# The seam between output projection and feed-forward, rearranged: first weights earlier, late tiles later, pair sums from kept values

## The chip, the cores and the metric

The kernel runs on one core of one Trainium2 chip. The metric is the device time of the whole program in microseconds (us), the median of several runs. One run of it was taken with the hardware profiler; all rows below are of that run.

## The reference

A step through a trunk of two layers, for 256 context tokens and 1024 latent tokens, which the kernel holds together as 1280 tokens in ten tiles of 128 (tiles 0 and 1 are context). Each layer has a mixer (layer 0 gMLP and attention, layer 1 neighbourhood attention) and then a feed-forward part; around each stand RMS norms, shift, scale and gate. What matters here is the end of the mixer and the start of the feed-forward part:

```
y  = mixer_out @ w_out                              # output projection, 1024 x 1024
x  = x + gate * rms_norm(y, norm_mix_post)
h  = rms_norm(x, norm_ffn_pre) * (1 + scale) + shift
g, u = split(h @ ffn_w_in)
out = (silu(g) * u) @ ffn_w_out
```

## The kernel before, in words

**Numbers.** Every matrix product in full precision is three products of rounded operands: a value is split into a high part (a CAST, L173 on VectorE (DVE) or L175 on ScalarE (ACT)) and a low part, the rest (TENSOR_TENSOR, L176, on GpSimd (POOL) or DVE). `hh` and `hl` hold the high and low parts of the normed, transposed tokens.

**Output projection** (`out_proj`, L1125). The tiles come in the order 4, 5, 6, 7, 8, 9, 2, 3, 0, 1; the last two, 0 and 1, are called late. `pipeline` runs four stages over them, each some steps behind the first: `load` (layer 0: the mixer's output is loaded and split, ACT L175 and POOL L176 of 128x1024), `product` (TensorE (PE), L190 to L192, 48 matmuls in layer 0 and 30 in layer 1, into one of two PSUM tiles A), `cols` and `norms`. `norms` is a chain of small steps on three engines, and I name it by its lines: sum of squares of y (ACT L353, then DVE L213), its root (POOL L214, a power, which I call the pow), gate and scale (DVE L431, which also frees A), the sum with x (DVE L432), then a second sum of squares (ACT L353), a second pow (POOL L214), and the normed tile `xh`, called hat here (DVE L359).

`cols` calls `prenorm_pair` (L382). PE transposes the hat in eight pieces (L394), ACT applies scale and shift to each (L397), and the result is split into `hh` and `hl`. The feed-forward products work on pairs of tiles, even and odd, and need sums over the pair. So the odd tile's `cols` has a pair chain behind it: POOL L403 (b - a), the splits, DVE L406 twice (a minus the even tile's high part, then minus its low part), POOL L408, L409 and L410 (the last two again with the even tile's high and low parts), and three stores to `t_d`. `cols` of a tile comes 2 steps behind `load` in layer 0 and 3 steps in layer 1. For the late tiles it is left out there and called inside `ffn`. The code of `out_proj` is put in order by the framework's scheduler, engine by engine.

**Feed-forward** (`ffn`, L1185). A block product is 12 matmuls (`three`, L1183) over four chunks of a weight block and a set of tiles: set 0 is the tiles 4 to 9 (128x384), set 1 the tiles 0 to 3 (128x256). Seven products make one output block; four of them, 1, 5, 2 and 3 (`FREE`), use `hh` and `hl` as they are. I write (m, i, s) for the product i of block m and set s. The first ones are (0,1,0), (0,5,0), (0,2,0), (0,3,0) and then (1,1,0) to (1,3,0). Their weights are loaded (L1213), combined (`weight_sums`) and split (ACT L175, POOL L176). `collect` takes a product out of its PSUM bank, first of all with an ACT COPY (L1266 for i = 1, L1274 for i = 5, L1277 for i = 2 the Silu). Here (0,2,0) adds onto the bank of (0,1,0), so it needs that bank's copy. The order inside `ffn` is written by hand: `at(p, ...)` gives each step a place, and `weave` runs them in the order of p on every engine. The late tiles' `cols` are at 0.04 and 1.45, the products start at 0.3.

Every engine works its instructions off in the program's order, so an instruction that waits holds those behind it on the same engine.

Of the kernel before, what the change touches and what calls it, by code (L numbers as in the profile page):

```python
# [49 lines left out]
def trunk_kernel(ctx: ExitStack, tc: tile.TileContext, A: dict, O: dict):  # L50
# [330 lines left out]

    def prenorm_pair(t, xh, l, w, lo, make, wide):  # L382


# [799 lines left out]

    def ffn(l, ubase, xsrc, dst, extra, before, after=()):  # L1185


# [27 lines left out]
        def weight_sums(m):  # L1215
# [13 lines left out]
            eng.tensor_tensor(s2, s1, g[:, 0], op=ALU.subtract)  # L1229
            if m == 0:  # L1230
                weights(m, 3)
                POOL.tensor_tensor(s3, g[:, 0], u[:, 0], op=ALU.subtract)
# [774 lines left out]
```

## Time and profile before

| | |
|---|---|
| median of 3 runs | 3361.82 us (3358.36 to 3364.49) |
| profiled run | 3360.7 us, span 3358.9 us |
| PE busy | 3166.4 us, 94% of the span, 18370 matmuls |
| DVE, POOL, ACT busy | 58%, 54%, 42% |
| granted clock of PE, mean | 0.974 |

The span is the time from the first to the last instruction of the profiled run. A row of a timeline reads: start in us, duration in us, engine, line and operation, tile written <- tiles read, shapes, count, and in brackets how long the engine had been idle before and which instruction ended that idle time. The granted clock 1.00 is full speed, 2.4 GHz; 0.5 is the lower level of 1.2 GHz; a mean between the two is a mix of stretches at either.

The out_proj and the first products of layer 0 lie at about 590 to 765 us, those of layer 1 at about 2370 to 2503 us.

### The profile page before, as it was taken

How to read it: one execution, taken by the hardware profiler on the slowest of the kernel's cores; microseconds unless marked ns; L12 is line 12 of the kernel's file. 1: busy time of each engine (PE TensorE's matmuls, PEld its weight loads, DVE VectorE, ACT ScalarE, POOL GpSimd, SP SyncE). 2: the span in 40 equal slices, each digit the busy share in tenths (PEclk: the TensorE clock that was granted, in tenths of full speed). 3: DMA queues.
4: the chain of work that ended last, by engine and by line, in shares of the span. 5: the costliest groups of instructions: out<-in, count | busy, mean ns of one | idle time of the engine just before them, and what ended most of it. 6: DMA issues, size and time to landing. Idle time of an engine off the chain costs nothing. (4 is left out here: it accounts for less than half of the span.)

```text
span 3358.9 us, 48818 instructions
## 1 busy us (share of the span) xinstructions
PE 3166.4 (94%) x18370; PEld 2785.2 (83%) x18370; DVE 1933.6 (58%) x3446; ACT 1404.4 (42%) x2935; POOL 1801.9 (54%) x1359
## 2 busy tenths in 40 slices
PE   7899999979999999999899999998869999999998
PEld 4688877759999999887778888887769999998877
DVE  4689988445667665444656666666666322224444
ACT  3478843433222223112456656566442333332121
POOL 4667765567656657434443433335376655565340
PEclk8999999989999999999999999999979999999999
DMA  6200134444233334223211111123443121223233
GB/s 228 78 17 26 45 99 151 140 133 136 101 113 114 130 124 131 89 85 126 106 49 46 48 47 50 46 67 105 135 138 123 62 82 62 69 84 119 83 119 119
DMA packets 167880, 321.14 MB, mean 96 GB/s; under 512 B 13518, under 2 KB 93262, under 8 KB 167644
## 3 DMA queue, kind: packets, MB, share of 16 engines
q1 hardware_dynamic: 167644, 318.03, 29.2%
q8 instruction: 144, 2.36, 0.3%
q14 instruction: 92, 0.75, 0.1%
HBM read 245.46 MB, written 72.52 MB: 95 GB/s over the span
## 5 line engine op out<-in xcount | busy, mean ns | idle before, releaser
L176 POOL TENSOR_TENSOR w<-raw,w 128x512 fp32r<-128x512 f32 (+1 forms) x303 | 463.5, 1540 | 372.9 <-ACT w L175 370.7
L1183 PE MATMUL B<-hh,w 128*128 128x384 f32 (+1 forms) x2112 | 523.2, 323 | 35.0 <-ACT s L1277 17.3
L1183 PE MATMUL A<-s,w 128*128 128x384 f32 (+1 forms) x3168 | 489.7, 310 | 6.1 <-DVE s L1269 6.0
L1183 PEld LDWEIGHTS A<-s,w 128*128 128x128 f32 x3168 | 474.3, 188 | 13.8 <-DVE s L1269 6.7
L1183 PEld LDWEIGHTS B<-hh,w 128*128 128x128 f32 x2112 | 376.9, 192 | 41.2 <-ACT s L1277 18.0
L175 ACT CAST w<-raw 128x512 fp32r<-128x512 f32 (+1 forms) x306 | 201.3, 688 | 459.8 <-DVE raw L1229 282.7
L1183 PE MATMUL B<-hl,w 128*128 128x384 f32 (+1 forms) x1056 | 339.7, 322 | 0.0
L477 PE MATMUL B<-c,s 128*128 128x128 f32 x1344 | 208.9, 279 | 26.7 <-DVE raw L459 14.3
L191 PE MATMUL B<-w,hh 128*128 128x512 f32 x552 | 220.2, 399 | 13.7 <-POOL w L176 13.7
L322 DVE SCALAR_TENSOR_TENSOR t<-s,c,t 128x512 f32<-128x512 f32 x196 | 216.0, 1148 | 25.7 <-DMA s<-mod_w 25.6
L190 PE MATMUL B<-w,hh 128*128 128x512 f32 x552 | 221.2, 401 | 8.4 <-DVE s L1404 8.4
L214 POOL TENSOR_TENSOR sm<-sm,c 128x1 f32<-128x1 f32 (+2 forms) x110 | 86.1, 783 | 266.3 <-DVE sm L213 264.6
L1404 DVE TENSOR_TENSOR s<-s,B 128x512 f32<-128x512 f32 x192 | 132.0, 687 | 161.9 <-PE B L192 161.9
L176 POOL TENSOR_TENSOR hl<-raw,hh 128x640 fp32r<-128x640 f32 (+1 forms) x84 | 127.9, 1526 | 174.3 <-ACT hh L175 166.5
L192 PE MATMUL B<-w,hl 128*128 128x512 f32 x552 | 219.8, 398 | 0.0
L190 PE MATMUL C<-hh,w 128*128 128x512 f32 (+1 forms) x576 | 213.1, 370 | 3.2 <-ACT s L135 1.2
L477 PEld LDWEIGHTS B<-c,s 128*128 128x128 f32 x1344 | 157.4, 142 | 67.6 <-DVE raw L459 17.5
L493 DVE TENSOR_TENSOR t<-B,t 128x512 fp32r<-128x512 f32 (+2 forms) x216 | 127.5, 590 | 143.8 <-ACT t L487 129.8
L192 PE MATMUL C<-hh,w 128*128 128x512 f32 (+1 forms) x576 | 205.9, 357 | 0.3 <-POOL w L176 0.3
L191 PE MATMUL C<-hl,w 128*128 128x512 f32 (+1 forms) x576 | 205.0, 356 | 0.0
L1183 PEld LDWEIGHTS B<-hl,w 128*128 128x128 f32 x1056 | 202.6, 192 | 0.0
L849 POOL TENSOR_TENSOR s<-s,sm 128x640 f32<-128x640 f32 x128 | 156.7, 1254 | 64.4 <-DVE sm L847 45.1
(361 smaller groups left out, 7891.1 us busy)
## 6 DMA issues: line engine op xcount, KB each, us to landing
raw<-wall SPq DMA_DIRECT2D x147, 512.0 KB, 3.6
s<-mod_w SPq DMA_DIRECT2D x56, 512.0 KB, 5.5
raw<-gu_d SPq DMA_DIRECT2D x88, 320.0 KB, 2.8
gu_d<-s SPq DMA_DIRECT2D x44, 384.0 KB, 3.1
raw<-x_d SPq DMA_DIRECT2D x30, 512.0 KB, 3.7
raw<-mod_w SPq DMA_DIRECT2D x24, 512.0 KB, 3.8
gu_d<-s SPq DMA_DIRECT2D x44, 256.0 KB, 3.3
w<-wall SPq DMA_DIRECT2D x22, 512.0 KB, 3.6
```

Of the source, the lines that this page charges most:

```text
L175: ACT.copy(hi, src)
L176: (eng or DVE).tensor_tensor(lo, src, f32(hi), op=ALU.subtract)
L190: PE.matmul(out, sh, mh, start=i == 0, stop=False)
L191: PE.matmul(out, sh, ml, start=False, stop=False)
L192: marks["PE"] = PE.matmul(out, sl, mh, start=False, stop=i == n - 1)
L214: POOL.tensor_tensor(r, v, mhalf[:, 0:n], op=ALU.pow)
L322: DVE.scalar_tensor_tensor(total[c], r[:, b], cond[:, k + b, c : c + 1], total[c], op0=ALU.mult, op1=ALU.add)
L477: PE.transpose(tr[:, at : at + P], self.p[a][:, col : col + P], ident)
L493: DVE.tensor_tensor(tl[:, 0:n], tr[:, 0:n], f32(th[:, 0:n]), op=ALU.subtract)
L849: POOL.tensor_tensor(p[:, c], p[:, c], z.to_broadcast([P, 640]), op=ALU.mult)
L1183: PE.matmul(out, x, z, start=start and i + j == 0, stop=i == n - 1 and j == 2, skip_group_check=True)
L1404: DVE.tensor_tensor(yt, yt, part, op=ALU.add)
```

## The change

Five things change, in both layers.

1. `out_proj` calls `ahead` within the product of the last tile: the first weight block is loaded there, and its weights 1, 5 and 2 are made there, so that the scheduler may set them among the work of the output projection. `ffn` becomes a generator that hands out `ahead`, and `ffn_behind` joins the two.
2. `cols` comes 3 steps behind `load` in both layers (it was 2 in layer 0).
3. In the hand-written order the first products stand at 0.0 (0.3 before), ahead of the late tiles' `cols`, which go to 0.71 and 2.45. The remaining sums of the first weights (`first_sums`) are made at 0.96, three of the four on DVE. Loads and splits of the pair sums move as shown.
4. Where `keep` is set (layer 1; in layer 0 the late tiles only) the even tile's values are kept, so one DVE L413 takes the place of two L406, and one POOL L417 that of L409 and L410.
5. The low part of b (the odd tile's second half) is always made on POOL; the low part of block 1's weights 5 and 3 goes to DVE.

Lines move by about ten: L403 becomes L409, L406 becomes L413, L408 becomes L415, L409 and L410 become L419 and L420 (or L417), L419 becomes L429, L431 becomes L441, L1183 becomes L1195, L1266 becomes L1289.

```diff
-    def prenorm_pair(t, xh, l, w, lo, make, wide):
+    def prenorm_pair(t, xh, l, w, lo, keep, wide):
...
             split(hh[:, :, rows(t)], hl[:, :, rows(t)], xh, lo, DVE)
+            if keep:
+                st["even"] = xh
             return
...
-        POOL.tensor_tensor(more[:, 0], b, a, op=ALU.subtract)
-        split(hh[:, 4:8, rows(t)], hl[:, 4:8, rows(t)], b, lo, DVE)
-        for x in (hh, hl):
-            DVE.tensor_tensor(a, a, f32(x[:, 0:4, rows(t - 1)]), op=ALU.subtract)
+        POOL.tensor_tensor(more[0], b, a, op=ALU.subtract)
+        split(hh[:, 4:8, rows(t)], hl[:, 4:8, rows(t)], b, POOL, DVE)
+        even = st.pop("even") if keep else None
+        for x in [even] if keep else (f32(hh[:, :, rows(t - 1)]), f32(hl[:, :, rows(t - 1)])):
+            DVE.tensor_tensor(a, a, x[:, 0:4], op=ALU.subtract)
         split(hh[:, 0:4, rows(t)], hl[:, 0:4, rows(t)], a, lo, DVE)
         POOL.tensor_tensor(b, b, a, op=ALU.subtract)
-        POOL.tensor_tensor(more[:, 1], f32(hh[:, 4:8, rows(t - 1)]), b, op=ALU.subtract)
-        POOL.tensor_tensor(more[:, 1], more[:, 1], f32(hl[:, 4:8, rows(t - 1)]), op=ALU.add)
+        if keep:
+            POOL.tensor_tensor(more[1], even[:, 4:8], b, op=ALU.subtract)
+        else:
+            POOL.tensor_tensor(more[1], f32(hh[:, 4:8, rows(t - 1)]), b, op=ALU.subtract)
+            POOL.tensor_tensor(more[1], more[1], f32(hl[:, 4:8, rows(t - 1)]), op=ALU.add)
...
+            if t == OUT_ORDER[-1]:
+                ahead()
...
-            prenorm_pair(t, st.pop(("xh", t)), l, 1, DVE if early else POOL, wt if early and t not in late else s5, t in late)
+            prenorm_pair(t, st.pop(("xh", t)), l, 1, DVE if early or t in late else POOL, early or t in late, t in late)
-        pipeline(OUT_ORDER, (0, load), (1, product), (3 if early else 2, lambda t: t in late or cols(t)), (1, norms))
+        pipeline(OUT_ORDER, (0, load), (1, product), (3, lambda t: t in late or cols(t)), (1, norms))
...
+        def first_sums():
+            g, u, s0 = st["gu", 0, 0], st["gu", 0, 1], st["s", 0]
+            DVE.tensor_tensor(s0[6], s0[5], g[:, 0], op=ALU.subtract)
+            weights(0, 3)
+            DVE.tensor_copy(s0[4], u[:, 1])
+            POOL.tensor_tensor(s0[7], g[:, 0], u[:, 0], op=ALU.subtract)
...
-            split(o[:, 0], o[:, 1], src, POOL)
+            split(o[:, 0], o[:, 1], src, DVE if m == 1 and i in (5, 3) else POOL)
+        def ahead():
+            weights_load(0)
+            weights(0, 1)
+            weight_sums(0)
+        yield ahead
...
-        at(0.04, before[0])
-        at(0.22, weights_load, 1)
-        p = 0.3
+        at(0.71, before[0])
+        at(0.96, first_sums)
+        at(0.97, weights_load, 1)
+        p = 0.0
...
-        at(1.45, before[1])
+        at(2.45, before[1])
...
-            at(1.7 + 0.25 * j, weights, 1, i)
+            at(2.55 + 0.45 * j, weights, 1, i)
...
-            at(0.5 + 0.7 * j, sums_load, i, h, 0)
-            at(2.6 + 0.7 * j, sums_split, i, h, 0)
+            at(1.2 + 0.7 * j, sums_load, i, h, 0)
+            at(3.6 + 0.6 * j, sums_split, i, h, 0)
```

How it moves instructions shows at three places. First POOL in the output projection of layer 0, in the kernel before. s_1118 is tile 5's hat, both L214 are tile 6's pows, and the last row is the split of a later tile's mixer output.

```order
L214 TENSOR_TENSOR sm_6483<-sm_6482,c_68 128x1
L403 TENSOR_TENSOR s_1126_6465<-s_1118_6388 128x512
L176 TENSOR_TENSOR hl_73<-s_1118_6388,hh_72 128x4x128
L408 TENSOR_TENSOR s_1118_6388<-s_1118_6388 128x512
L176 TENSOR_TENSOR hl_73<-s_1118_6388,hh_72 128x4x128
L409 TENSOR_TENSOR s_1126_6465<-hh_72,s_1118_6388 128x512
L214 TENSOR_TENSOR sm_6494<-sm_6493,c_68 128x1
L410 TENSOR_TENSOR s_1126_6465<-s_1126_6465,hl_73 128x512
L176 TENSOR_TENSOR s_1139_6502<-raw_6499,s_1138_6501 128x1024
```

The chain of the same tile 5 in the changed kernel, where s_1116 is its hat and both L214 are tile 7's pows:

```order
L409 TENSOR_TENSOR t_1141_6542<-s_1116_6368 128x512
L176 TENSOR_TENSOR hl_73<-s_1116_6368,hh_72 128x4x128
L415 TENSOR_TENSOR s_1116_6368<-s_1116_6368 128x512
L176 TENSOR_TENSOR hl_73<-s_1116_6368,hh_72 128x4x128
L419 TENSOR_TENSOR t_1142_6543<-hh_72,s_1116_6368 128x512
L420 TENSOR_TENSOR t_1142_6543<-t_1142_6543,hl_73 128x512
L214 TENSOR_TENSOR sm_6561<-sm_6560,c_68 128x1
L214 TENSOR_TENSOR sm_6572<-sm_6571,c_68 128x1
L176 TENSOR_TENSOR s_1155_6580<-raw_6577,s_1154_6579 128x1024
```

Before, the first of the two pows stands ahead of the odd tile's pair chain and the second within it; now both stand behind all of the chain.

The same holds for the chains of the tiles 7, 9 and 3. PE's order follows: before, a tile's eight transposes stood between two products and no other tile's with them; now, between the products of the tiles 8 and 9, the eight of tile 6 and the first four of tile 7 stand (B_6731 from s_1152, tile 7's hat), and so the product of tile 9 waits for tile 7's hat.

Second, POOL in the output projection of layer 1, before (the L403 is the one of tile 7; the L214 behind it is the pow of tile 9's y; L419 makes the context tiles' gate):

```order
L403 TENSOR_TENSOR w_23262<-s_3678_23134 128x512
L214 TENSOR_TENSOR sm_23280<-sm_23279,c_68 128x1
L408 TENSOR_TENSOR s_3678_23134<-s_3678_23134 128x512
L409 TENSOR_TENSOR w_23262<-hh_72,s_3678_23134 128x512
L410 TENSOR_TENSOR w_23262<-w_23262,hl_73 128x512
L419 TENSOR_TENSOR w_23370<-w_23370,raw_23371 128x1024
```

and in the changed kernel, where s_3683 is tile 7's hat:

```order
L409 TENSOR_TENSOR t_3702_23263<-s_3683_23135 128x512
L176 TENSOR_TENSOR hl_73<-s_3683_23135,hh_72 128x4x128
L415 TENSOR_TENSOR s_3683_23135<-s_3683_23135 128x512
L417 TENSOR_TENSOR t_3703_23264<-s_3667_23050,s_3683_23135 128x512
L429 TENSOR_TENSOR w_23370<-w_23370,raw_23371 128x1024
L214 TENSOR_TENSOR sm_23280<-sm_23279,c_68 128x1
```

The pow of tile 9 moved from behind L403 to behind L417 and the gate's product, L429; the chain has one instruction fewer of its own and one split of b more.

Third, ACT at the start of the first products of layer 0 in the changed kernel. s_1226 and s_1243 are the hats of the tiles 3 and 0, A_7095 is y of tile 1, and the L1289 is the copy that (0,2,0) waits for.

```order
L397 ACTIVATE s_1226_6994<-B_7163,c_74 128x128 x2
L175 CAST w_7156<-t_1249_7151 128x512
L175 CAST w_7159<-raw_7144 128x512
L397 ACTIVATE s_1226_6994<-B_7163,c_74 128x128 x2
L397 ACTIVATE s_1243_7091<-A_7243,c_74 128x128
L353 ACTIVATE t_1259_7195,sm_7196<-A_7095,c_70 128x1024
L397 ACTIVATE s_1243_7091<-A_7243,c_74 128x128 x7
L353 ACTIVATE t_1264_7206,sm_7207<-s_1263_7202,c_70 128x1024
L1289 COPY s_1272_7262<-B_7217 128x384
```

In the kernel before the copy (L1266 there) stands here, behind tile 0's eight L397 but with tile 1's two sums of squares well ahead:

```order
L353 ACTIVATE t_1239_7113,sm_7114<-s_1238_7109,c_70 128x1024
L353 ACTIVATE t_1246_7173,sm_7174<-A_7124,c_70 128x1024
L353 ACTIVATE t_1251_7184,sm_7185<-s_1250_7180,c_70 128x1024
L175 CAST w_7207<-t_1259_7202 128x512
L175 CAST w_7210<-raw_7195 128x512
L1226 COPY t_1262_7205<-raw_7197 128x512
L175 CAST w_7216<-raw_7195 128x512
L397 ACTIVATE s_1243_7120<-A_7220,c_74 128x128 x8
L175 CAST w_7271<-raw_7239 128x512
L175 CAST w_7274<-raw_7239 128x512
L1266 COPY s_1274_7277<-B_7243 128x384
```

Now the copy stands behind tile 1's second sum of squares, that is, behind all of tile 1's `norms`.

## Rows read from the trace of the kernel before

**Rows 1.** Windows: us, busy us of PE, PEld, DVE, ACT, POOL, PEclk, DMA share, GB/s.

```profile
603.81:615.75 11.94, 11.94 (x58) 9.84 (x56) 6.31 (x6) 6.18 (x13) 5.86 (x4) 1.00 0.41 134
631.55:645.18 13.63, 13.63 (x56) 11.25 (x57) 6.15 (x6) 5.09 (x11) 7.94 (x5) 0.87 0.53 161
661.03:676.77 15.74, 15.10 (x56) 11.87 (x57) 6.14 (x6) 5.08 (x11) 7.94 (x5) 0.78 0.50 151
719.25:765.05 45.80, 26.07 (x113) 24.61 (x114) 19.56 (x17) 19.80 (x40) 36.96 (x29) 0.78 0.45 149
2460.00:2503.20 43.20, 23.68 (x97) 21.85 (x97) 23.34 (x20) 18.71 (x38) 33.68 (x24) 0.71 0.44 146
```

**Rows 2.** Timeline of PE, layer 0: start, us, engine, line, tiles [idle before <-releaser].

```profile
631.55 1.86 PE L394 MATMUL B<-c,s 128*128 128x128 f32 x8 [3.69 <-DVE sm L213]
...
661.03 1.09 PE L394 MATMUL B<-c,s 128*128 128x128 f32 x8 [3.74 <-DVE sm L213]
...
723.54 1.64 PE L394 MATMUL A<-c,s 128*128 128x128 f32 x8 [4.29 <-DVE sm L213]
...
739.23 0.69 PE L1183 MATMUL B<-hh,w 128*128 128x384 f32 x1 [6.24 <-ACT s L1266]
...
756.09 0.69 PE L1183 MATMUL B<-hh,w 128*128 128x384 f32 x1 [8.01 <-ACT s L1277]
```

**Rows 3.** Timeline of POOL, layer 0, 646 to 663 us.

```profile
646.91 0.55 POOL L214 TENSOR_TENSOR sm<-sm,c 128x1 f32<-128x1 f32 x1 [4.15 <-DVE sm L213]
649.57 1.48 POOL L403 TENSOR_TENSOR s<-s 128x512 f32<-128x512 f32 x1 [2.11 <-ACT s L397]
651.01 1.30 POOL L176 TENSOR_TENSOR hl<-s,hh 128x512 fp32r<-128x512 f32 x1
...
654.73 1.48 POOL L408 TENSOR_TENSOR s<-s 128x512 f32<-128x512 f32 x1 [2.42 <-issue]
...
657.43 1.26 POOL L409 TENSOR_TENSOR s<-hh,s 128x512 f32<-128x512 f32 x1
...
660.38 2.81 POOL L176 TENSOR_TENSOR s<-raw,s 128x1024 fp32r<-128x1024 f32 x1
```

**Rows 4.** Timeline of ACT, layer 0, 645 to 650 us.

```profile
645.44 1.11 ACT L353 ACTIVATE t<-A,c 128x1024 bf16<-128x1024 f32 x1 [6.44 <-PE A L192]
...
646.54 2.89 ACT L397 ACTIVATE s<-B,c 128x128 f32<-128x128 f32 x8
```

**Rows 5.** Timeline of DVE, layer 0, 649 to 654 us.

```profile
649.81 1.28 DVE L431 SCALAR_TENSOR_TENSOR s<-A,sm,s 128x1024 f32<-128x1024 f32 x1
651.08 1.78 DVE L406 TENSOR_TENSOR s<-s,hh 128x512 f32<-128x512 f32 x1
652.78 1.21 DVE L432 TENSOR_TENSOR s<-s,raw 128x1024 f32<-128x1024 f32 x1
```

**Rows 6.** Timeline of DVE, layer 1: L431 of tiles 7 and 3.

```profile
2397.15 1.28 DVE L431 SCALAR_TENSOR_TENSOR s<-A,sm,w 128x1024 f32<-128x1024 f32 x1 [0.44 <-POOL sm L214]
...
2438.83 1.28 DVE L431 SCALAR_TENSOR_TENSOR s<-A,sm,w 128x1024 f32<-128x1024 f32 x1 [0.44 <-POOL sm L214]
```

**Rows 7.** Timeline of PE, layer 1.

```profile
2398.58 0.47 PE L190 MATMUL A<-s,hh 128*128 128x512 f32 x1 [2.40 <-DVE s L431]
...
2407.13 1.04 PE L394 MATMUL B<-c,s 128*128 128x128 f32 x8
...
2455.17 1.94 PE L394 MATMUL A<-c,s 128*128 128x128 f32 x8 [6.91 <-DVE s L359]
...
2467.23 0.69 PE L1183 MATMUL B<-hh,w 128*128 128x384 f32 x1 [6.05 <-ACT w L175]
...
2477.68 0.44 PE L1183 MATMUL B<-hh,w 128*128 128x384 f32 x1 [3.40 <-ACT s L1266]
...
2495.06 0.69 PE L1183 MATMUL B<-hh,w 128*128 128x384 f32 x1 [9.31 <-ACT s L1277]
```

**Rows 8.** Timeline of POOL, layer 1: the gate's product.

```profile
2422.19 2.87 POOL L419 TENSOR_TENSOR w<-w,raw 128x1024 f32<-128x1024 f32 x1
```

More of the change, by code (lines that the diff above doesn't have):

```diff
@@ L399, in prenorm_pair @@
             split(hh[:, :, rows(t)], hl[:, :, rows(t)], xh, lo, DVE)
+            if keep:
+                st["even"] = xh
             return
         a, b = xh[:, 0:4], xh[:, 4:8]
-        more = make([P, 2, 4, P])
-        POOL.tensor_tensor(more[:, 0], b, a, op=ALU.subtract)
-        split(hh[:, 4:8, rows(t)], hl[:, 4:8, rows(t)], b, lo, DVE)
-        for x in (hh, hl):
-            DVE.tensor_tensor(a, a, f32(x[:, 0:4, rows(t - 1)]), op=ALU.subtract)
+        if wide:
+            more = s5([P, 2, 4, P])
+            more = [more[:, i] for i in range(2)]
+        else:
+            more = [t2([P, 4, P]) for _ in range(2)]
+        POOL.tensor_tensor(more[0], b, a, op=ALU.subtract)
[3 more added lines that the diff above has]
+            DVE.tensor_tensor(a, a, x[:, 0:4], op=ALU.subtract)
         split(hh[:, 0:4, rows(t)], hl[:, 0:4, rows(t)], a, lo, DVE)
         POOL.tensor_tensor(b, b, a, op=ALU.subtract)
-        POOL.tensor_tensor(more[:, 1], f32(hh[:, 4:8, rows(t - 1)]), b, op=ALU.subtract)
-        POOL.tensor_tensor(more[:, 1], more[:, 1], f32(hl[:, 4:8, rows(t - 1)]), op=ALU.add)
-        for i, src in enumerate((b, more[:, 0], more[:, 1])):
+        if keep:
+            POOL.tensor_tensor(more[1], even[:, 4:8], b, op=ALU.subtract)
+        else:
+            POOL.tensor_tensor(more[1], f32(hh[:, 4:8, rows(t - 1)]), b, op=ALU.subtract)
+            POOL.tensor_tensor(more[1], more[1], f32(hl[:, 4:8, rows(t - 1)]), op=ALU.add)
+        for i, src in enumerate((b, *more)):
             SP.dma_start(t_d[l][i][:, :, rows(t // 2)], src)
@@ L1122, in trunk_kernel, with out_proj @@
     finish(mod_part)
-    def out_proj(l, w, xsrc, dst, early=None):
+    def out_proj(l, w, xsrc, dst, early=None, ahead=None):
         w0, w1 = w[:4], w[4:]
@@ L1225, in weight_sums @@
                 weights(m, 2)
-                ACT.copy(a22, u[:, 1])
             else:
                 DVE.tensor_tensor(s3, g[:, 0], u[:, 0], op=ALU.subtract)
[L1229 to L1232, printed above, removed]
+                DVE.tensor_tensor(s2, s1, g[:, 0], op=ALU.subtract)
+        def first_sums():
[4 more added lines that the diff above has]
+            POOL.tensor_tensor(s0[7], g[:, 0], u[:, 0], op=ALU.subtract)
         def weights(m, i):
@@ L1237, in weights @@
             if i == 3:
-                (DVE if m else POOL).tensor_tensor(g[:, 1], g[:, 1], st["s", m][6], op=ALU.subtract)
+                DVE.tensor_tensor(g[:, 1], g[:, 1], st["s", m][6], op=ALU.subtract)
             src = {1: g[:, 0], 2: g[:, 1], 3: g[:, 1]}[i] if i < 4 else st["s", m][i]
             st["w", m, i] = o = wt([P, 2, 512], F32R)
-            split(o[:, 0], o[:, 1], src, POOL)
+            split(o[:, 0], o[:, 1], src, DVE if m == 1 and i in (5, 3) else POOL)
[4 more added lines that the diff above has]
+        yield ahead
         banks = {}
@@ L1303, in both @@
             at(p + (SHORT if s else LONG) + 0.12, collect, m, i, s)
-        at(-0.02, weights_load, 0)
-        at(0.0, weights, 0, 1)
-        at(0.02, weight_sums, 0)
-        at(0.04, before[0])
-        at(0.22, weights_load, 1)
-        p = 0.3
+        at(0.71, before[0])
+        at(0.96, first_sums)
+        at(0.97, weights_load, 1)
+        p = 0.0
         for i in FREE:
@@ L1313, in ffn @@
             p += LONG
-        at(1.45, before[1])
-        at(0.95, weights, 1, 1)
-        at(1.0, weights, 1, 2)
-        at(1.6, weight_sums, 1)
+        at(2.45, before[1])
+        at(1.35, weights, 1, 1)
+        at(1.95, weights, 1, 2)
+        at(2.0, weight_sums, 1)
         for j, i in enumerate((5, 3)):
-            at(1.7 + 0.25 * j, weights, 1, i)
+            at(2.55 + 0.45 * j, weights, 1, i)
         for i in FREE:
@@ L1493, in ffn, with ffn_behind @@
             finish(steps)
-    late_cols = out_proj(0, early_w, lambda t: A["x"][rows(t), :], x_d[0])
+    def ffn_behind(l, *args):
+        k = args.index(None)
+        before = []
+        steps = ffn(l, *args[k + 1 : k + 5], before, *args[k + 5 :])
+        before += out_proj(l, *args[:k], ahead=next(steps))
+        finish(steps)
     FIRST = {0: 0, 7: 640}
@@ L1659, in trunk_kernel @@
     first_units = []
-    ffn(
-        0, U_F0, x_d[0], lambda t: x_d[1][rows(t), :], mods_of((1, 0), (1, 1), (0, 5), (1, 2), (1, 3), (1, 4)), late_cols,
+    ffn_behind(
+        0, early_w, lambda t: A["x"][rows(t), :], x_d[0], None,
+        U_F0, x_d[0], lambda t: x_d[1][rows(t), :], mods_of((1, 0), (1, 1), (0, 5), (1, 2), (1, 3), (1, 4)),
         [first_products(CH[0]), by_turns(first_products(CH[1]), itertools.chain(first_head(0), first_loads()))],
@@ L1889, in trunk_kernel @@
         finish(gen)
-    late_cols = out_proj(1, o_w, lambda t: grid_rows(x_d[1], t), x_d[2], o_sums)
     def last(t):
         return O["yp"][rows(t), :] if t < 2 else O["ys"].rearrange("(r j c) d -> j r c d", j=8, c=8)[t - 2]
-    ffn(1, U_F1, x_d[2], last, mods_of((1, 5)), late_cols)
+    ffn_behind(1, o_w, lambda t: grid_rows(x_d[1], t), x_d[2], o_sums, None, U_F1, x_d[2], last, mods_of((1, 5)))
 def _units_k(w, n):
```

## The prediction

> **What bounds the kernel now.** The table above has PE busy 94% of the span, so only its idle time and its lower clock can be won or lost. The program order differs only around the two seams, so I read those. I took the windows first [rows 1]: an undisturbed step of layer 0's output projection lasts 11.94 us, all of it PE work at granted clock 1.00, while steps around a wait last 13.63 and 15.74 us at 0.87 and 0.78. The first products are worse: PE is busy in 26.07 of 45.80 us in layer 0 and in 23.68 of 43.20 us in layer 1, at 0.78 and 0.71. Then PE's timeline, for what ends the waits. In layer 0 [rows 2] eight transposes wait 3.69 us for the hat of tile 6, and 3.74 for that of tile 8; at the seam stand waits of 4.29, 6.24 and 8.01 us. In layer 1 [rows 7] a product waits 2.40 us for L431 (its PSUM tile A is not free), and at the seam stand 6.91, 6.05 and 9.31. Last POOL, DVE and ACT around such a wait [rows 3 to 5], for what is late: the hat needs two pows, and POOL has them among the pair chain's long instructions. POOL's queue there is what the change rearranges.
>
> **Output projection of layer 0.** Before, products end at 627.86 (tile 7: 631.55 less 3.69), 657.29 (tile 9) and 719.25 (tile 1) [rows 2]. After, with `cols` a step later, one set of transposes fewer stands ahead of tile 7's product: it ends about 1.0 us earlier, at 626.8 (a set takes 1.09 at full clock in [rows 2]).
>
> From there the way to tile 9's product is this. Tile 5's first four transposes and its eight L397 (2.89 [rows 4]): 626.8 + 0.6 + 2.9 = 630.3. Then POOL's pair chain: L409 1.48, split 1.30, L415 1.48, split 1.30, L419 and L420 1.26 each, 8.1 in all; in the trace POOL also stood 2.42 us within a chain [rows 3], beside DVE instructions of the same data [rows 5]. That bounds the chain by 8.1 and 10.5; both cases are equally near, so I take 9.25: 639.6. Only now come the pow of y (0.55 [rows 3]), L441 1.28 and L442 1.21 [rows 5], the second sum of squares (1.11 [rows 4] and some 0.2 of readout), the second pow 0.55, and the split of tile 9's mixer output 2.81 [rows 3]: 647.3, with three or four hand-overs of 0.1 to 0.2, 647.9. Meanwhile tile 8's product has ended at 638.8 and the transposes of tile 6 at 639.8, so PE stands about 6 us for tile 7's hat and 1.5 more for the split. The rest of the product needs 10.5 (11.94 less a set of transposes, less what ran before the split was there): 658.4, plus c for the lower clock after the wait.
>
> The next two odd tiles repeat it: tile 7's chain holds the split of tile 3's mixer output, tile 9's that of tile 1. One period is 0.6 + 2.9 + 9.25 + 7.4 + 0.6 + 10.5 = 31.3 + c. For c the trace has 13.63 - 11.94 = 1.7 and 15.74 - 11.94 = 3.8 [rows 1], of which the second holds 0.6 more idle time; with nothing lost it is 0. I take 1.6. Tile 1's product then ends at 626.8 + 3 x 32.9 = 725.5 against 719.25: **+6** (with 8.1 and 0: -2; with 10.5 and 3.2: +14). So the waits of 3.7 go, and what is late next is the odd tile's pow.
>
> One rule of the Trainium skill bears on the chain ("SBUF — State Buffer", section "Who interferes with whom"): a VectorE instruction with both inputs in SBUF and a GpSimd instruction that reads SBUF block one another whole. The trace agrees: L406 on 512 columns took 1.78 beside POOL's split, longer than L432's 1.21 on 1024 [rows 5]. By that rule the b split, newly on POOL in layer 1, delays the L413 beside it by 0.5 us a chain, some 1.5 us for three chains, and the forecast would be 3373.
>
> **Seam of layer 0**, from the end Z of tile 1's product. The first weights are now ready, so (0,1,0) and (0,5,0) follow at once; the waits of 4.29 and the small ones behind it go. But (0,2,0) needs the bank's copy, and on ACT that stands behind all of tile 1's `norms`, whose pow stands behind tile 3's pair chain on POOL. Z + 0.5 (second half of tile 3's transposes) + 2.7 (four L397 and two casts) + 9.25 + 0.55 + 1.28 + 1.21 + 1.3 + 0.6 for the copy and 1.3 of hand-overs: Z + 18.7. Before it was 739.23 - 719.25 = 20.0 [rows 2]. So the front of the seam gives back 1.3. Behind it, tile 1's transposes now come after (1,1,0), and the cast for (1,5,0) stands behind their L397 on ACT: 2.89 + 0.6 for the copy + 0.6 for the cast + the low part, now on DVE at 0.7 to 1.8, some 5.5 us of new wait. The wait of 8.01 shrinks by less, since the copies of (0,2,0) and (0,3,0) still come one behind the other. I put all PE waits at 12.5 + 1.5 + 5.5 + 2 = 21.5 against 45.80 - 26.07 = 19.7 [rows 1]: **+2** (-1 with the last two terms hidden, +5 with another stretch at the lower clock).
>
> **Output projection of layer 1.** Here `cols` was 3 behind already. L431 of tile 7 started at 2397.15 [rows 6], its pow within tile 5's chain; now the pow is behind L417: one split (1.30) and the rest of the chain later, less the dropped L410: 2399.9. Tile 9's product begins when A is free: 2399.9 + 1.28 + 0.15 = 2401.3, and lasts 8.55 as before [rows 7], since the wait ahead of it is longer: 2409.9. Then 0.6 + 2.9 + 1.3 (a sum of squares stands between tile 7's L397) + the chain of 5.6 (1.48, 1.30, 1.26, 1.5) + the gate's 2.87 [rows 8] + 0.55 + 0.4: L441 of tile 9 at 2424.1. And again, with 1.4 + 7.7 for tile 3's product (8.55, or 6.8 where the clock is granted) and no gate: 20.6, L441 of tile 3 at 2444.7 against 2438.83 [rows 6]: **+6** (+3 with full clock, +7.5 with the lock above).
>
> **Seam of layer 1**, from Y, the start of tile 3's L441. Tile 1's product, tile 3's transposes and (0,1,0) follow without a wait, the last at Y + 9.5; before it came 18 us behind Y, after the 6.91. (0,5,0) still waits: its cast needs the weight sum on POOL, behind the split of tile 3's b, behind eight L397: Y + 9.5 + 2.9 + 1.3 + 1.3 + 1.3 + 1.3 = Y + 17.6, its low part at 20. (0,2,0) needs the copy behind tile 1's norms, and their pow stands behind tile 3's chain: Y + 31.5 (24.6 for the pow, then 1.28, 1.2, 1.3, the late L397 2.5, the copy 0.6), against 2477.68 - 2438.83 = 38.9 [rows 6, 7]. Of these 7.4 about half is given back as in layer 0: set 0's free products end at Y + 61 instead of 2503.20 - 2438.83 = 64.4 [rows 1, 6]: **-3.5** (-6 to -2).
>
> What else changes I cost at nothing. On SP the two weight loads go ahead of the last tiles' transfers, and the late tiles' three stores each come later; the loads of the pair sums that read them come later too, and the products that need these sums lie behind all free products of both sets, well over 20 us on. DVE's new splits stand where PE works on the products before. Without that cover a split costs its 0.7 to 1.8 us once, a late transfer as much as it is late.
>
> **Sum:** 6 + 2 + 6 - 3.5 = +10.5. The profiled run had 3360.7 us (span 3358.9), 1.1 below the median, so I predict about 3371 to 3372.
>
> **Rivals.**
> *The first products fill the waits.* If ACT gets to the copies before tile 1's norms are done, (0,1,0), (0,5,0) and (0,2,0) run back to back. In layer 1 that saves 6.91, 6.05 and most of the 9.31 with their stretches at 0.71, some 18; in layer 0 4.29 and 6.24, some 10; with the output projections at their lower ends (-2, +3): -27, 3335. Half of it gives 3348. For it: the weights are indeed ready early. Against: each engine keeps its order, and the copy stands behind the norms. It decides once POOL's chain of tile 3 ends before tile 1's product does; I have it 12 us later in layer 0.
> *The waits only move.* Chain of 8.1 and little clock loss in layer 0 (+0), seam +1, layer 1 +3 and -4: within 6 us of before, 3361. For it: the cycle of 31.3 is close to the old one, (719.25 - 627.86) / 3 = 30.5.
> *The chain is slow.* 10.5 per chain and c of 3: layer 0 +13, the rest +6: 3381. For it: 2.42 of waiting within a chain was seen.
>
> **Chances.** My forecast 0.41, the slow chain 0.12, moved waits 0.22, filled waits 0.25. A measurement tells about 0.2% (6.7 us) from no change. Faster 0.26 (the filled waits and a little), same 0.24, slower 0.50. For 8 in 10 the range must reach into the filled waits' milder half: 3349 to 3383; the forecast's own is 3364 to 3379.
>
> **What would show it.** In the new profile: POOL's L214 behind L420 with PE's transposes of tile 7 waiting some 6 us; tile 1's product ending near 725; in layer 1 L441 of tile 3 near 2452 (2444.7 and the 8 us of layer 0); (0,2,0) ended by ACT's L1289 in both seams. I am wrong if POOL's pow starts before L419, if PE's waits around the products of the tiles 9 and 3 are under 3 us, or if the seams lose more than 10 us of their idle time.

## The result, and the profile after

The changed kernel takes 3382.82 us (median of 4, 3380.9 to 3384.48), the kernel before 3360.28 in the same comparison: 1.0063 times as long, 95% interval 1.0048 to 1.0078. It is slower, as forecast, and by about twice the forecast amount (22.5 us against 10.5 to 11); 3382.8 lies at the upper end of the stated range and above the forecast's own 3364 to 3379.

The page of the changed kernel, its span and PE's share:

```profile
span 3382.3 us, 48785 instructions
PE 3164.1 (94%) x18370; PEld 2782.2 (82%) x18370; DVE 1914.6 (57%) x3447; ACT 1402.6 (41%) x2933; POOL 1779.4 (53%) x1348
```

PE does the same matmuls in 3164 busy us; the span has grown by 23.4. Where it grew is read from the starts of the same instructions in both traces (us; E6 and E1 are the ends of tile 6's and tile 1's products in layer 0, C the first product of set 1):

| stretch | before | after | difference | forecast |
|---|---|---|---|---|
| start to E6, layer 0 | 615.8 | 610.7 | -5.0 | -1.0 |
| E6 to E1, output projection | 103.5 | 112.2 | +8.7 | +7.3 |
| E1 to C, seam | 47.1 | 49.3 | +2.2 | +2 |
| C to the 601st matmul of the feed-forward | 76.7 | 78.9 | +2.2 | 0 |
| from there to tile 4's transposes, layer 1 | 1536.6 | 1540.3 | +3.7 | 0 |
| these to tile 1's product's end | 67.7 | 79.8 | +12.1 | +6 |
| seam of layer 1 | 57.1 | 52.6 | -4.5 | -3.5 |
| C to the 601st matmul | 75.0 | 78.2 | +3.2 | 0 |
| the rest | 779.4 | 780.3 | +0.9 | 0 |

The fifth row and the last hold no instruction whose order changed; from the first only tile 4's eight transposes are gone, which now stand behind E6 (the forecast's 1.0). Further runs (below) put the first at 611.4 to 617.0 for kernels with these transposes behind E6, and at 613.8 in a second run of the kernel before, so single traces can't tell some 3 us there. That second run has 101.6, 48.1 and 76.9 in the next three rows, and 68.0, 57.5 and 76.3 in those of layer 1; so 1 to 2 us of a row aren't told from scatter either.

PE's timeline in layer 0 of the changed kernel, its waits of more than 1 us from tile 9's product on (this answers to [rows 2]):

```profile
641.99 0.45 PE L394 MATMUL B<-c,s 128*128 128x128 f32 x1 [6.37 <-DVE s L359]
...
673.82 0.79 PE L190 MATMUL A<-s,s 128*128 128x512 f32 x1 [4.64 <-ACT s L175]
...
676.69 0.79 PE L192 MATMUL A<-s,s 128*128 128x512 f32 x1 [1.65 <-POOL s L176]
...
709.26 0.45 PE L394 MATMUL B<-c,s 128*128 128x128 f32 x1 [6.34 <-DVE s L359]
...
741.46 0.69 PE L1195 MATMUL B<-hh,w 128*128 128x384 f32 x1 [12.50 <-ACT s L1289]
...
756.30 0.45 PE L1195 MATMUL B<-hh,w 128*128 128x384 f32 x1 [3.87 <-ACT w L175]
...
762.57 1.01 PE L1195 MATMUL B<-hh,w 128*128 128x384 f32 x2 [5.66 <-DVE w L176]
...
792.66 4.85 PE L1195 MATMUL A<-s,w 128*128 128x384 f32 x14 [4.10 <-DVE s L1292]
```

The waits of 3.7 are gone, and in their place stand 6.37 for tile 7's hat, 4.64 and 1.65 for the split of the mixer's output, 6.34 for tile 3's hat. At the seam (0,2,0) waits 12.50 for the copy, (1,5,0) 3.87 and 5.66 for its cast and its low part. POOL at the first of these waits (it answers to [rows 3]):

```profile
626.26 1.54 POOL L409 TENSOR_TENSOR t<-s 128x512 f32<-128x512 f32 x1 [4.70 <-ACT s L397]
627.76 1.30 POOL L176 TENSOR_TENSOR hl<-s,hh 128x512 fp32r<-128x512 f32 x1
630.48 1.48 POOL L415 TENSOR_TENSOR s<-s 128x512 f32<-128x512 f32 x1 [1.42 <-DVE s L413]
631.91 1.30 POOL L176 TENSOR_TENSOR hl<-s,hh 128x512 fp32r<-128x512 f32 x1
633.17 1.30 POOL L419 TENSOR_TENSOR t<-hh,s 128x512 f32<-128x512 f32 x1
634.55 1.26 POOL L420 TENSOR_TENSOR t<-t,hl 128x512 f32<-128x512 f32 x1
635.78 0.55 POOL L214 TENSOR_TENSOR sm<-sm,c 128x1 f32<-128x1 f32 x1
640.51 0.55 POOL L214 TENSOR_TENSOR sm<-sm,c 128x1 f32<-128x1 f32 x1 [4.18 <-DVE sm L213]
641.25 2.81 POOL L176 TENSOR_TENSOR s<-raw,s 128x1024 fp32r<-128x1024 f32 x1 [0.20 <-ACT s L175]
```

Tile 5's whole chain, L409 to L420, stands ahead of tile 7's first pow at 635.78; the second comes at 640.51, the split at 641.25, and PE goes on at 641.99. POOL's queue isn't alone in this. On DVE the step ahead of the pow, L213, stands behind the chain's steps too, at 630.71, though ACT had the sum ready at 627.3. In more_s5, the first of the experiments, it runs as soon as ACT has it. Both rows, changed kernel first:

```profile
630.71 0.15 DVE L213 TENSOR_SCALAR sm<-sm 128x1 f32<-128x1 f32 x1
```

```profile
627.06 0.15 DVE L213 TENSOR_SCALAR sm<-sm 128x1 f32<-128x1 f32 x1 [2.07 <-ACT t L353]
```

Layer 1 of the changed kernel, PE's waits in the output projection and at the seam, answering to [rows 7]:

```profile
2413.58 0.76 PE L190 MATMUL A<-s,hh 128*128 128x512 f32 x1 [5.66 <-DVE s L441]
...
2439.08 0.76 PE L190 MATMUL A<-s,hh 128*128 128x512 f32 x1 [6.98 <-DVE s L441]
...
2461.33 0.77 PE L190 MATMUL A<-s,hh 128*128 128x512 f32 x1 [4.53 <-DVE s L441]
...
2479.47 0.69 PE L1195 MATMUL B<-hh,w 128*128 128x384 f32 x1 [5.33 <-ACT w L175]
...
2493.20 0.69 PE L1195 MATMUL B<-hh,w 128*128 128x384 f32 x1 [7.67 <-ACT s L1289]
...
2508.36 0.69 PE L1195 MATMUL B<-hh,w 128*128 128x384 f32 x1 [3.87 <-ACT w L175]
2514.62 1.01 PE L1195 MATMUL B<-hh,w 128*128 128x384 f32 x2 [5.26 <-DVE w L176]
```

Here A is not free: three waits for L441 of 5.66, 6.98 and 4.53, where before stood five for L431: 2.40 [rows 7], 1.83, two under 1 and the longest of them:

```profile
2430.37 0.63 PE L190 MATMUL A<-s,hh 128*128 128x512 f32 x1 [2.81 <-DVE s L431]
```

Windows around the idle time and the product behind it, in the changed kernel (a step of layer 0 without a wait first; columns as in [rows 1]):

```profile
610.71:622.65 11.94, 11.94 (x58) 9.85 (x57) 6.30 (x6) 6.18 (x13) 5.86 (x4) 1.00 0.45 133
634.59:656.61 22.02, 15.48 (x61) 12.10 (x60) 7.68 (x10) 9.65 (x20) 11.40 (x8) 0.77 0.45 134
2408.00:2424.00 16.00, 10.42 (x37) 8.40 (x38) 9.98 (x14) 4.81 (x12) 4.64 (x5) 0.79 0.37 113
2434.00:2448.01 14.01, 8.93 (x30) 7.18 (x31) 8.09 (x10) 2.94 (x6) 4.72 (x5) 0.76 0.52 161
2456.80:2471.02 14.22, 9.70 (x31) 7.72 (x31) 10.52 (x12) 5.46 (x13) 5.37 (x6) 0.76 0.34 112
```

A step without a wait still takes 11.94 us at 1.00. Over wait and product together the clock is 0.76 to 0.79, and a product of 30 matmuls, some 6.9 us at full clock, takes 9.7 (2413.58 to the next transposes at 2423.31).

### The profile page after: what moved, and what is told of

Its sections match the earlier page's. It is cut to its first block, busy times and chain, and to the rows that moved or that the text cites. A ratio compares the mean times of both kernels' runs of the same rounds, so it can differ in the third digit from the quotient of the medians.

```text
span 3382.3 us, 48785 instructions
## 1 busy us (share of the span) xinstructions
PE 3164.1 (94%) x18370; PEld 2782.2 (82%) x18370; DVE 1914.6 (57%) x3447; ACT 1402.6 (41%) x2933; POOL 1779.4 (53%) x1348
## 4 chain that ended last, share of the span: by engine, by line
PE 46%; DVE 6%; ACT 4%; POOL 4%; issue 4%; DMA 2%; POOLq 0%; DVEq 0%; SPq 0%; ACTq 0%
PE A L1195 8%; PE B L1195 8%; PE B L191 3%; PE B L192 3%; PE B L190 3%; PE C L190 3%; PE C L192 3%; PE C L191 2%; PE A L190 2%; PE C L1195 2%; PE A L191 2%; PE A L192 2%; PE B L487 2%; PE B L521 2%; POOL w L176 1%
## 5 line engine op out<-in xcount | busy, mean ns | idle before, releaser
L1195 PE MATMUL B<-hh,w 128*128 128x384 f32 (+1 forms) x2112 | 522.0, 323 | 47.2 <-ACT s L1289 20.2
L1195 PE MATMUL A<-s,w 128*128 128x384 f32 (+1 forms) x3168 | 493.1, 312 | 8.5 <-DVE s L1292 8.2
L1195 PEld LDWEIGHTS A<-s,w 128*128 128x128 f32 x3168 | 477.6, 190 | 16.4 <-DVE s L1292 8.8
L1195 PEld LDWEIGHTS B<-hh,w 128*128 128x128 f32 x2112 | 375.4, 191 | 54.4 <-ACT s L1289 20.7
L1195 PE MATMUL B<-hl,w 128*128 128x384 f32 (+1 forms) x1056 | 339.1, 321 | 0.0
L214 POOL TENSOR_TENSOR sm<-sm,c 128x1 f32<-128x1 f32 (+2 forms) x110 | 84.9, 772 | 286.3 <-DVE sm L213 285.0
L1195 PEld LDWEIGHTS B<-hl,w 128*128 128x128 f32 x1056 | 202.4, 192 | 0.0
```

What stands on the lines that cost most here:

```text
L214: POOL.tensor_tensor(r, v, mhalf[:, 0:n], op=ALU.pow)
L1195: PE.matmul(out, x, z, start=start and i + j == 0, stop=i == n - 1 and j == 2, skip_group_check=True)
```

## The experiments

All on one core, each beside runs of the kernel before. Ratios are to the kernel before; "out0" is E6 to E1 and "out1" tile 4's transposes to tile 1's product's end, from each run's trace.

| kernel | us | ratio, 95% | out0 | out1 |
|---|---|---|---|---|
| changed kernel | 3382.8 | 1.0063 (1.0048 to 1.0078) | 112.2 | 79.8 |
| more_s5 | 3372.3 | 1.0032 (1.0020 to 1.0043) | 104.2 | 75.0 |
| old_pair | 3367.8 | 1.0017 (1.0008 to 1.0026) | 104.1 | 67.7 |
| norms_first | 3360.0 | 0.9996 (0.9987 to 1.0005) | 103.1 | 65.9 |
| lag_2 | 3386.8 | 1.0078 (1.0065 to 1.0090) | 111.8 | 78.6 |
| norms_first_split_dve | 3349.6 | 0.9963 (0.9950 to 0.9977) | 91.2 | 65.6 |
| before_order_only | 3349.5 | 0.9961 (0.9947 to 0.9974) | 84.0 | 66.9 |
| block1_w5_early | 3383.8 | 1.0062 (1.0050 to 1.0075) | 111.7 | 78.4 |
| sums_block2_late | 3382.6 | 1.0059 (1.0046 to 1.0072) | 112.1 | 78.4 |
| all_four | 3350.1 | 0.9966 (0.9954 to 0.9979) | 89.6 | 67.4 |
| tile1_cols_later | 3349.6 | 0.9963 (0.9950 to 0.9975) | 89.6 | 65.6 |

**What put the pow behind the chain.** The two pair results take two of the five buffers of t2, and `sumsq` takes a buffer there too (`junk, ss = t2([P, n], BF16), sm(1)`). The first edit moves the pair results only:

```diff
-        if wide:
-            more = s5([P, 2, 4, P])
-            more = [more[:, i] for i in range(2)]
-        else:
-            more = [t2([P, 4, P]) for _ in range(2)]
+        more = s5([P, 2, 4, P])
+        more = [more[:, i] for i in range(2)]
```

> The changed kernel with one edit: the odd tile's two pair results (more) come from the pool s5, as before, not from t2, which also serves the sums of squares. In the program POOL's first pow then stands ahead of layer 0's pair chain again, and in layer 1 one instruction earlier. Theory A (the shared pool put the pow behind the chain, and that is what costs): PE's waits of 6.4, 4.6 and 6.3 us in layer 0's output projection go with their half-clock tails, so the stretch from tile 7's product to tile 1's falls from 100 to 75 to 85 us; layer 1 gains 3 to 6 us; in all 3355 to 3363 us. Rival B (the cost is the amount of work put on POOL, b's low part above all, wherever the pow stands): within 3 us of the changed kernel, 3380 to 3386.

Measured 3372.3: half of the loss is gone, 8.0 us in layer 0 (of 8.7) and 4.8 in layer 1 (of 12.1), by a change of a buffer's pool alone. What it moves is more than the pow: in layer 0 the steps of `norms` on POOL, ACT and DVE stand ahead of the pair chain or within it again, and on PE no tile's transposes are cut in two by a product. B is refuted; A's cause, the order, holds, its sizes don't (from tile 7's product to tile 1's 92.2, not 75 to 85). In layer 0 PE still waits 4.9 us three times, now for the split of the mixer's output, which stands behind the chain on POOL as it did; the first of them:

```profile
643.91 0.63 PE L192 MATMUL A<-s,s 128*128 128x512 f32 x1 [4.88 <-POOL s L176]
```

**The order by itself.**

```diff
-        pipeline(OUT_ORDER, (0, load), (1, product), (3, lambda t: t in late or cols(t)), (1, norms))
+        pipeline(OUT_ORDER, (0, load), (1, product), (1, norms), (3, lambda t: t in late or cols(t)))
```

> The changed kernel with one edit in out_proj's pipeline: the stage norms is emitted ahead of the stage cols. The same instructions; POOL's pows stand ahead of the pair chain or within it, in both layers, and no transposes of the next tile ahead of a product. Theory A (order of the pows): both output projections lose their waits, layer 0 from 100 to 72 to 82 us, layer 1 from 79.6 (tile 4's transposes to tile 1's product) to 58 to 66, and tile 1's norms come earlier at the seams: 3335 to 3355 us, faster than the kernel before. Rival B (amount of POOL work): 3378 to 3385.

Measured 3360.0, no slower than the kernel before, with every instruction of the change still there. In layer 1 the expected 58 to 66 came (65.9). In layer 0, counted from tile 7's product as the expectation does, 91.2 came instead of 72 to 82 (100.2 in the changed kernel; six steps of 11.94 are 71.6): a wait was left. POOL and PE of this run at that wait:

```profile
637.13 1.47 POOL L415 TENSOR_TENSOR s<-s 128x512 f32<-128x512 f32 x1 [0.69 <-DVE sm L213]
638.56 0.55 POOL L214 TENSOR_TENSOR sm<-sm,c 128x1 f32<-128x1 f32 x1
639.08 1.31 POOL L176 TENSOR_TENSOR hl<-s,hh 128x512 fp32r<-128x512 f32 x1
640.35 1.76 POOL L419 TENSOR_TENSOR t<-hh,s 128x512 f32<-128x512 f32 x1
642.18 1.26 POOL L420 TENSOR_TENSOR t<-t,hl 128x512 f32<-128x512 f32 x1
643.41 2.34 POOL L176 TENSOR_TENSOR s<-raw,s 128x1024 fp32r<-128x1024 f32 x1
```

```profile
645.80 0.50 PE L192 MATMUL A<-s,s 128*128 128x512 f32 x1 [4.05 <-POOL s L176]
```

Tile 7's first pow now runs ahead of the chain, at 630.10, and the second (638.56) within it, and PE waits 4.05 for the split of 643.41 behind L420. This kernel keeps the pair results in t2, so that it was the order that cost, not a want of buffers. The edit moves all steps of `norms` at once; what the pow's place on POOL and L213's on DVE are worth each was not tried apart.

**The pair chain as it was.** prenorm_pair and its call word for word from the kernel before, the rest of the change kept.

> The changed kernel with prenorm_pair as it was (two DVE and two POOL instructions instead of the one each from kept values, b's low part by the old rule, pair results from s5 or w); cols still 3 steps behind, first weights ahead, late tiles late. Theory A: the pow stands within the chain in both layers; layer 0 as with the pair results from s5 (75 to 85 us), layer 1 near the 67.5 of the kernel before; 3347 to 3358 us. Rival C (the 3 steps and the late tiles' new place cost): no better than 3375.

Measured 3367.8, above A's 3347 to 3358, below C's 3375. Layer 1 is exactly back (67.7), layer 0 as in more_s5. Which of the kept values, b's split on POOL and the pools makes the 7.3 us between more_s5 and this run in layer 1 was not tried apart; norms_first has all of them and 65.9, so with `norms` ahead none of them costs.

**The third step.**

```diff
-        pipeline(OUT_ORDER, (0, load), (1, product), (3, lambda t: t in late or cols(t)), (1, norms))
+        pipeline(OUT_ORDER, (0, load), (1, product), (3 if early else 2, lambda t: t in late or cols(t)), (1, norms))
```

> The changed kernel with cols 2 steps behind load in layer 0 again. In the program both pows still stand behind the whole pair chain. Theory A: the wait stays, and moves from the next but one product to the next, so layer 0 does not get better: 3380 to 3392 us. Rival C (the third step is what costs in layer 0): layer 0's loss of 7.6 goes, 3374 to 3377.

Measured 3386.8, as A had it. PE's three waits for a hat, 3.7 before, are 7.1 to 7.2 here, the first of them:

```profile
632.32 1.97 PE L394 MATMUL B<-c,s 128*128 128x128 f32 x8 [7.13 <-DVE s L359]
```

So the third step did no harm; the pair chain ahead of the steps of `norms` did.

**The last long instruction in the queue.** norms ahead of cols, and:

```diff
-            split(oh, ol, of, POOL)
+            split(oh, ol, of, DVE)
```

> The kernel with norms emitted ahead of cols, and one edit more: in layer 0 the low part of the mixer's output (128x1024) is made on DVE, not POOL. In the run before this one PE still waited 4.05, 3.97 and 3.97 us there, ended by that split, which stands behind the pair chain in POOL's queue. Theory A (POOL's queue order is the whole of it): these waits and their tails go, tile 4's transposes to tile 1's product fall from 103 to 95.5 to 98 us (eight steps of 11.94), 3352 to 3356 us in all. Rival (DVE takes POOL's place: its split delays gate and hat): 3358 to 3364 us.

Measured 3349.6, faster than the kernel before; out0 falls from 103.1 to 91.2 (the expected figures counted from tile 4's transposes, the same point), below the 95.5 I had for no wait at all, which counted one step too many. The waits of 4 become 1.4 to 2.2:

```profile
641.01 0.50 PE L192 MATMUL A<-s,s 128*128 128x512 f32 x1 [1.47 <-DVE s L176]
...
692.89 0.51 PE L192 MATMUL A<-w,s 128*128 128x512 f32 x1 [2.16 <-DVE s L176]
```

**The same order without the change.** The kernel before with three edits: 3 steps in both layers, norms ahead of cols, the split on DVE.

> The kernel before with three small edits in out_proj and nothing else of the change: cols 3 steps behind in both layers, norms emitted ahead of cols, the mixer output's low part on DVE. It asks what the change's seam (first weights ahead, late tiles later) and its kept values are worth once POOL's order is put right; the kernel with the whole change and the same order has 3349.6 us. Theory A with the stages seen so far (seam and what follows cost 2 to 5 us in all against before): 3343 to 3350 us, the seam is worth nothing. Rival E (the seam saves its 3 to 5 us of layer 1 once the order is right): 3352 to 3357.

Measured 3349.5, the same as with the whole change (3349.6). Once POOL's order is right, the earlier first weights, the late tiles' new place and the kept values together are worth nothing that can be measured. Output projection and seam trade: out0 84.0 and a seam of 50.3 here, 91.2 and 47.6 there; in layer 1 66.9 and 60.5 against 65.6 and 55.3.

**The new waits of the seam.** Two edits on the changed kernel, one at a time. First block 1's weight 5 ahead of tile 1's cols:

```diff
-            at(2.55 + 0.45 * j, weights, 1, i)
+            at((2.44, 3.0)[j], weights, 1, i)
```

> The changed kernel with one edit at the seam: block 1's weight 5 is made just ahead of tile 1's cols (2.44, not 2.55), so its cast stands ahead of tile 1's eight L397 on ACT. Theory A (the waits of 3.87 and 5.66 us in layer 0 and 3.87 and 5.26 in layer 1, new against the kernel before, come from that place): they fall to 2 or less together, 5 to 8 us a layer with their tails, 3367 to 3373 us. Rival D (POOL is behind with its work and gives it back at the bound products): 3377 to 3384.

Measured 3383.8. The waits of 3.87 and 5.66 are gone, and a new one of 7.67 stands ahead of the next product, (1,2,0). ACT and PE there:

```profile
765.30 0.62 ACT L175 CAST w<-raw 128x512 fp32r<-128x512 f32 x1 [6.81 <-DVE raw L1255]
765.83 0.47 ACT L1289 COPY s<-B 128x384 f32<-128x384 f32 x1
```

```profile
766.35 0.69 PE L1195 MATMUL B<-hh,w 128*128 128x384 f32 x1 [7.67 <-ACT s L1289]
```

The copy of (1,1,0) at 765.83 stands behind the cast of weight 3, which waits 6.81 for a sum on DVE. A is refuted. What was meant by D (POOL's work returned at the bound products) isn't what the rows show either: the wait moved to the next instruction of the same queue. Second, block 2's sums later:

```diff
-        at(9.2, weight_sums, 2)
+        at(9.8, weight_sums, 2)
```

> The changed kernel with one edit: the sums of block 2's weights come at 9.8, not 9.2. In the changed kernel PE waits 4.10 us in each layer for a collect on DVE, which stands behind a weight sum, which waits 4.31 us for a split on POOL (3.02 and 2.41 before). Theory A: that wait of PE falls below 1 us and its slow tail goes, 3 to 5 us a layer, 3373 to 3377 us. Rival D (POOL's backlog only moves the wait to the next product): 3380 to 3385.

Measured 3382.6. DVE and PE of the changed kernel at that place, and PE of this run:

```profile
791.44 0.69 DVE L1241 TENSOR_TENSOR raw<-t,raw 128x512 f32<-128x512 f32 x1 [4.31 <-POOL w L176]
792.05 0.55 DVE L1292 TENSOR_TENSOR s<-A,s 128x384 f32<-128x384 f32 x1
```

```profile
799.21 4.10 PE L1195 MATMUL A<-s,w 128*128 128x384 f32 x14 [3.08 <-DVE s L1302]
```

In the changed kernel the collect L1292 stands behind L1241, which waits 4.31 for POOL's split. With the sums later, the wait of 4.10 becomes one of 3.08 for the collect L1302, not below 1 as A had it: about the 3.02 that the kernel before has there. The stretch C to the 601st matmul shortens by 1.9 and 1.7 us, to 77.0 and 76.6, about what the second trace of the kernel before has (76.9 and 76.3); the whole shows nothing beyond its interval.

**All four edits.**

> The changed kernel with four edits: norms ahead of cols, the mixer output's low part on DVE, block 1's weight 5 ahead of tile 1's cols, block 2's sums late. If each wait is its own (theory A) the gains add: 3330 to 3345 us, faster than the kernel before by 0.5 to 1%. If POOL's amount of work bounds the seam (rival D): 3350 or more.

Measured 3350.1: the gains of norms and split stand, the two seam edits add nothing. They don't add up since they move waits, as the two runs before showed.

**Tile 1's cols later still**, on norms_first_split_dve:

```diff
-        at(2.45, before[1])
+        at(3.3, before[1])
```

> The kernel with norms ahead of cols and the split on DVE, and one edit more: tile 1's cols at 3.3, not 2.45, behind (1,1,0) and (1,5,0). Theory A (in the seam ACT's queue order sets the waits, 3.88 and 5.66 us in layer 0): they fall to 2 together, 3340 to 3346 us. Rival D (the wait moves on, as it did with block 1's weight 5 made earlier, to the next copy or to set 1's products): 3347 to 3353.

Measured 3349.6. The seam shortens by 4.7 us in each layer (42.9 and 50.6), and the stretch behind it grows by 4.3 and 4.6 (83.2 and 82.7), with a wait before the bound products that was 4.09:

```profile
768.38 3.89 PE L1195 MATMUL A<-s,w 128*128 128x384 f32 x11 [5.93 <-DVE s L1292]
```

That is the return that D described, shown in one pair of stretches.

**A second trace of the kernel before.**

> The kernel before once more, unchanged, for a second trace. Theory: the stretches outside the two seams differ between two runs of the same program by up to 4 us each (the start of layer 0's output projection lay between 599.8 and 605.5 us in the kernels so far, where nothing before it differs in order), so that the changed kernel's -4.2 before 586 us and part of its +3.7 between the seams are no effect of the change. If instead the start is again at 603.8 within 0.3, these are effects.

Measured 3359.3 in one run, and E6 at 613.8 against 615.8. The stretch between the layers took 1535.3, against 1536.6 in its first trace; all eleven other kernels, before_order_only with its untouched feed-forward too, lie at 1537.8 to 1541.4. So the start is scatter. The 1 to 4 us between the layers are more than the two traces of before differ by at the end of that stretch; but on the way the second is at one point 1.4 us behind the first and later 2.7 ahead, so two traces are too few to call them an effect, and their cause stays open.

## Why the prediction was right, and where its sizes were off

**The mechanism** of layer 0 was right to the step. Forecast: from tile 7's product's end to the pow 12.8 us, to the start of tile 9's remaining matmuls 21.1. Measured from 622.65: 13.1 (635.78) and 21.5 (644.12). The chain took 9.5 (626.26 to 635.78) where I had taken 9.25 between 8.1 and 10.5. The tile's hat as the releaser and 6 us of wait came as said at the tiles 7 and 3; in the period between, PE waited 4.64 and 1.65 for the two halves of the split. lag_2, more_s5 and norms_first show that it is the place of the steps of `norms`, the pow among them, and not the number of steps between the stages. That DVE's L213 stood behind the chain as well is not in the forecast; with the pow behind all of POOL's chain it cost nothing more.

**The tail, c.** In layer 0, 1.6 a period was about right: three periods took 100.2 (622.65 to 722.87), 33.4 each. The forecast's 31.3 without c has a slip: its 7.4 should be 7.7, as in the first period (639.6 to 647.3), which made the forecast 0.9 too low. With 7.7, and the chain at 9.5, a period is 31.8, and 1.6 is left for c. In layer 1 the forecast let a product behind the wait last 8.55 or less, because one had behind 2.40 of idle time [rows 7]. Behind 5.66, 6.98 and 4.53 it took 9.7, 8.9 and 9.7, at 0.76 to 0.79. L441 of the tiles 7, 9 and 3 came at 2412.15, 2437.65 and 2459.90; with layer 1 starting 11.7 later, the forecast's 2399.9, 2424.1 and 2444.7 were short by 0.5, 1.8 and 3.5, and tile 1's product, which I had counted at about the old length, by 2.7 more. That is the mis-sized term: +12.1 for +6. It came of taking the longest duration seen for the longest possible; the idle times forecast were longer than any in those rows.

**The lock.** That L413 blocks and is blocked beside POOL's split was cited from the Trainium skill ("SBUF — State Buffer", section "Who interferes with whom"); the trace agrees: in tile 5's chain of layer 1 L413 took 1.76 beside POOL's split, in tile 7's, begun while POOL stood idle, 0.68. POOL waited 0.68 for the slower one, where I had put 0.5 a chain:

```profile
2406.60 1.76 DVE L413 TENSOR_TENSOR s<-s,s 128x512 f32<-128x512 f32 x1 [1.19 <-POOL t L409]
...
2429.90 0.68 DVE L413 TENSOR_TENSOR s<-s,s 128x512 f32<-128x512 f32 x1
```

```profile
2406.52 1.29 POOL L176 TENSOR_TENSOR hl<-s,hh 128x512 fp32r<-128x512 f32 x1
2408.49 1.45 POOL L415 TENSOR_TENSOR s<-s 128x512 f32<-128x512 f32 x1 [0.68 <-POOL hl L176]
...
2430.12 1.62 POOL L176 TENSOR_TENSOR hl<-s,hh 128x512 fp32r<-128x512 f32 x1 [0.42 <-DMA raw<-gpost]
```

**What was costed at nothing.** "What else changes I cost at nothing" failed, though not at the pair sums that it spoke of: behind C the changed kernel loses 2.2 and 3.2 us (2.0 and 1.9 against the second trace of before). Some 1.1 of it in each layer is wait, by a collect on DVE behind a sum of block 2's weights that waits for POOL's split (4.10 for 3.02), and sums_block2_late, which moves that sum, comes back to about the second trace of before. The rest is PE's busy time at a lower granted clock. The windows of layer 0's stretch in the kernel before, the changed kernel and before_order_only:

```profile
766.35:843.08 76.73, 73.71 (x503) 71.49 (x501) 45.42 (x56) 27.63 (x56) 58.24 (x47) 0.98 0.37 123
```

```profile
772.17:851.09 78.92, 74.82 (x502) 72.60 (x500) 44.62 (x56) 28.90 (x58) 60.06 (x47) 0.96 0.36 120
```

```profile
748.22:826.24 78.02, 74.98 (x502) 72.76 (x500) 45.45 (x56) 27.64 (x56) 58.23 (x47) 0.96 0.37 121
```

before_order_only, with tile 1's pair chain in its old place, waits no longer there than the kernel before (3.04); its 78.0, and 77.7 in layer 1, are busy time at 0.96, where the kernel before has 0.98 and 1.00. Why the clock was lower there stays open. That tile 1's pair chain, now behind (1,1,0), makes POOL late is what tile1_cols_later speaks for, which moves it on again and loses 4.3 and 4.6 more.

**The seams.** In layer 0 (0,2,0) started at Z + 18.6 (741.46 - 722.87; forecast 18.7), in layer 1 at Y + 33.3 (2493.20 - 2459.90; 31.5), both ended by L1289. Layer 0's +2.2 for +2 is right as a sum, with some luck in its terms: the wait for (1,5,0)'s cast and low part was 9.5 (3.87 and 5.66) where the forecast had 5.5, and less than forecast stood beside it. Layer 1's -4.5 in the table is counted from E1, the forecast's -3.5 from Y. Counted from Y as well, to the end of set 0's free products, the seam took 62.6 against 64.4: -1.8, less than the forecast's -6 to -2; and the way from tile 4's transposes to Y grew by 9.3, not 6. Both go back to the tail above, since tile 1's longer product lies between Y and E1.

**The rivals.** "The first products fill the waits" decides only once tile 3's chain ends before tile 1's product. It did not: that chain began at 727.46, and the product had ended at 722.87; (0,2,0), its weights ready, waited 12.50 for the copy. "The waits only move" (3361) is out by the time itself. "The chain is slow" (3381) came nearest in sum, but by terms that were not measured: the chain took 9.5, not 10.5, and c was 1.6, not 3; what the forecast lacked lies in layer 1 and behind C. With the mis-sized tail and the nothing behind C, that the time still fell within the stated range, by 0.2 us, was luck. The first of the things that would have shown me wrong (a pow ahead of L419) did not come: POOL's row 635.78 stands behind L420.

## What to carry to other kernels

An in-order engine that does both long bulk steps and the short step of a chain should have the short one ahead; the place of the steps of `norms`, a pow of 0.55 us and an L213 of 0.15 us among them, decided some 23 us here (3382.8 to 3360.0), and a buffer pool shared between the two is enough to turn their order round. After every edit of buffers, read engine by engine what stands ahead of the short step. Where a wait is taken away, look at what stands next in the same queue: the three edits at the seams gained nothing in all, while two on what stands ahead of the steps of `norms` and behind them, on POOL above all, took 33 us (3382.8 to 3349.6).

## What the runs showed of the hardware

A product behind a wait costs more than the wait: in layer 1, 30 matmuls took some 6.9 us behind no wait or one under 1 us, 8.5 behind 2.40 and 2.81 us of idle time, 9.7 behind 4.53 and 5.66, so that the 5.66 cost 8.5 in all. The extra doesn't grow in step with the wait: behind 6.98 the product took 8.9. And two traces of one program differed by 2.0 us at E6 (615.8 and 613.8), and by up to 1.9 in a stretch of 100 us behind it.
